# Softmax sums from the value product, reciprocals spread over DRAM, and a narrow maxima row in the last attention

## The chip, the cores and the metric

The kernel runs on one core of one Trainium2 chip. The metric is the device time of one execution, in microseconds (us). The kernel before was timed three times; one further execution was recorded by the hardware profiler, and every row below comes from that one.

## The reference

The reference is two stacks of layers, one after the other, on a sequence of 512 positions and 1024 channels. The change touches only the last mixer of the second stack, a grouped-query attention whose 512 queries see 768 keys (256 of a context and the 512 of the sequence):

```python
def attend(q, k, v):
    q = q.reshape(bsz, lq, A_NKV, A_REP, A_HEADDIM)          # 4 key heads x 4 query heads x 64
    s = jnp.einsum('bqgrd,bkgd->bgrqk', q, k).astype(F32) * (A_HEADDIM ** -0.5)
    p = jax.nn.softmax(s, axis=-1).astype(v.dtype)
    o = jnp.einsum('bgrqk,bkgd->bqgrd', p, v)
    return o.reshape(bsz, lq, A_W)

o_lat = (ol * jax.nn.silu(gl)) @ out_w
```

There are 16 query heads of width 64. Queries and keys are normalised and rotated before this, and scores are large, so the kernel subtracts each query's maximum before the exponential.

## The kernel before

All of it is float32 work done as split products: an operand is kept as a high part (type `fp32r`) and a low part, and three products replace one (`mm3`, lines 229 to 231; `split`, lines 212 and 215). Weights are loaded by SP into one of three `wraw` buffers, split by ScalarE (`whi`, line 212) and by VectorE or, in this attention, GpSimd (`wlo`, line 215).

The last attention is a set of Python generators that are stepped by hand, so that pieces of several jobs alternate in the program. A scheduler then orders each engine's instructions. A chunk `c` is a pair of heads (e = 0 and 1) that share 128 rows; there are 8 chunks, hence 16 turns. In each turn of six steps run:

- `head(c, e)`: for each of 6 blocks of 128 keys, two products give scores minus maximum in PSUM tile `st` (lines 1352, 1353; the second one takes the row of maxima from `qb`). ScalarE takes the exponential twice, once rounded to `fp32r` (`ath`, line 1357) and once in float32 (`ap`, line 1358); VectorE subtracts (`atl`, line 1359). GpSimd adds the `ap` blocks to a running sum `asum` (lines 1362, 1364). Two steps later the block is multiplied with the values: `ath` by [high | low] values into all 128 rows of `po` (line 1370) and `atl` by the high values into 64 rows (lines 1369, 1372). At the end ScalarE and VectorE add both halves of `po` into `aout` (lines 1379, 1380). The first steps of the next turn finish the last two blocks.
- `maxima` of the next head: four times two products fill the one `mx` tile and VectorE reduces it to a column of `a_m` (lines 1328, 1329). VectorE then builds diagonal matrices `adg` of them (line 1332), one product with all-ones rows turns them into a row (line 1336), and ScalarE copies that row into `qb` (line 1337).
- a filler: the gate projection of this chunk (e = 0) or the query projection of the chunk after the next (e = 1), 24 products with `hh` each; towards the end the first output projections (`begin`).
- `finish(c - 1)`, in a turn with e = 0 from its third step: products of `asum` with a column of 2.0 (line 1389; 2, since `agate` holds twice the gate) give sums per query in PSUM tile `aux`, VectorE takes reciprocals (line 1392) and spreads them over a diagonal in `hsq` (line 1394), GpSimd multiplies gate and `aout` (line 1396), products with the identity give the reciprocals in all rows (line 1401), and VectorE multiplies and splits (lines 1402, 215).

PSUM has 8 banks here: one for `mm`, one for `aux`, two for `mx`, two for `st`, two for `po`. After the loop the banks are given out anew and the output projection runs (`fin`, lines 1449 onward): the last chunk's result `ol[7]` is wanted by the last of the eight row blocks of each of its products.

Of the kernel before, what the change touches and what calls it, by code (L numbers as in the profile page):

```python
# [12 lines left out]
F32 = mybir.dt.float32  # L13
F32R = mybir.dt.float32r
AF = mybir.ActivationFunctionType
# [131 lines left out]
class Kern:  # L147
# [1038 lines left out]
    def attention(self, hh, hl, mod):  # L1186
        nc, d = self.nc, self.d
        with ExitStack() as st:
# [11 lines left out]
            vs = ap.tile([P, 6, 2, 256], F32R, name="avs")  # L1200
# [9 lines left out]
            for e in range(2):  # L1210
                for b in range(2):
                    fill(kb[b][e], other[e], 0.0)
                    fill(kb[b][e], row[e], -1.0)
                    fill(qb[b][e], other[e], 0.0)
            tables = ap.tile([P, 2, S], F32, name="rope")
            nc.sync.dma_start(tables, d["rope"].rearrange("e p t -> p e t"))
            onesr = ap.tile([P, P], F32R, name="onesr")
            nc.vector.tensor_copy(onesr, self.ones)
            pick = ap.tile([P, 3], F32, name="two")
            self.two, double = pick[:, :2], pick[:, 2:]  # L1220
            nc.vector.memset(self.two, 0.0)
            nc.vector.memset(double, 2.0)
# [5 lines left out]
            gates, outs = {}, {}  # L1228

# [24 lines left out]
            def values(nb, o, ih, il):  # L1254

                w = [self.weights(d["a_v"][0][:, k * 1024 : (k + 1) * 1024]) for k in range(2)]
                for b in range(nb):
# [6 lines left out]
                    out = vs[:, o + b].rearrange("p g (e f) -> p g e f", f=64)  # L1264
                    self.split(ps[:, :256].rearrange("p (g e f) -> p g e f", g=2, e=2), out[:, :, 0:4:2], out[:, :, 1:4:2])
# [52 lines left out]
            with self.psum(1, 1), self.pool("mx", 1, space=PSUM) as mxp, \  # L1318
                    self.pool("st", 2, space=PSUM) as stp, self.pool("po", 2, space=PSUM) as pop:

                def maxima(c, e):

                    q, k = qa[c % 2][e], ka[c // 4][e]
                    m = self.sp.tile([P, 4], F32, name="a_m")
                    for b in range(4):
                        sc = mxp.tile([P, T], F32, name="mx")
                        for o in (slice(0, S), slice(S, T)):
# [3 lines left out]
                    dg = mp.tile([P, 4, P], F32R, name="adg", bufs=1)  # L1331
                    nc.vector.tensor_tensor(dg, self.ident[:, None, :].to_broadcast([P, 4, P]),
                                            m[:, :, None].to_broadcast([P, 4, P]), op=ALU.mult)
                    yield
                    bc = self.abank()
                    nc.tensor.matmul(bc, onesr, dg.rearrange("p b q -> p (b q)"), start=True, stop=True)
                    nc.scalar.activation(qb[c % 2][e][row[e]], bc[row[e]], AF.Copy)
                    yield

                def head(c, e):  # L1340

                    g, b = c // 4, c % 2
                    both, lead = slice(e * P, (e + 1) * P), slice(e * P, e * P + 64)
                    r = own[e]
                    po = pop.tile([P, S], F32, name="po")
                    total = mp.tile([P, S], F32, name=f"asum{e}", bufs=1)
                    parts = {}
                    for k in range(8):
                        if k < 6:
# [11 lines left out]
                            if k == 1:  # L1361
                                nc.gpsimd.tensor_tensor(total, first, p, op=ALU.add)
                            elif k > 1:
                                nc.gpsimd.tensor_tensor(total, total, p, op=ALU.add)  # L1364
                            first = p
                        if k > 1:
                            th, tl = parts.pop(k - 2)
                            if k == 7:
                                nc.tensor.matmul(po[:64], vs[:, 5, g, lead], tl, start=False, stop=False)
                            nc.tensor.matmul(po, vs[:, k - 2, g, both], th, start=k == 2, stop=k == 7)  # L1370
                            if k < 7:
                                nc.tensor.matmul(po[:64], vs[:, k - 2, g, lead], tl, start=False, stop=False)
                        if k < 7:
                            yield
                    if e == 0:
                        outs[c] = mp.tile([P, S], F32, name="aout", bufs=2), []
                    out, totals = outs[c]
                    totals.append(total)
                    nc.scalar.activation(out[r], po[other[e]], AF.Copy)
                    nc.vector.tensor_tensor(out[r], out[r], po[r], op=ALU.add)  # L1380
                    yield

                def finish(c):

                    out, totals = outs.pop(c)
                    st = self.abank()
                    for b in range(4):
                        for e, total in enumerate(totals):
                            nc.tensor.matmul(st[:, 2 * b + e : 2 * b + e + 1], total[:, b * P : (b + 1) * P], double,  # L1389
                                             start=True, stop=True)  # L1390
                    r = self.sp.tile([P, 8], F32, name="rs_r")
                    nc.vector.reciprocal(r, st[:, :8])
                    dg = mp.tile([P, S], F32, name="hsq", bufs=1).rearrange("p (b q) -> p b q", q=P)
                    nc.vector.tensor_copy(dg.rearrange("p b (e f) -> p (b e) f", e=2), r[:, :, None].to_broadcast([P, 8, 64]))  # L1394
                    t = gates.pop(c)
                    nc.gpsimd.tensor_tensor(t, t, out, op=ALU.mult)
                    yield
                    yield
                    bc = self.abank()
                    for b in range(4):  # L1400
                        nc.tensor.matmul(bc[:, b * P : (b + 1) * P], dg[:, b], self.ident, start=True, stop=True)
                    nc.vector.tensor_tensor(t, t, bc, op=ALU.mult)
                    ol[c] = low(c)
                    self.split(t, oh[c], ol[c])
                    yield
# [131 lines left out]
```

## Time and profile before

| | |
|---|---|
| median of three runs | 3234.89 us (3228.05 to 3239.75) |
| profiled execution, own time | 3230.24 us |
| its span | 3228.5 us |
| TensorE busy (products) | 3075.5 us, 95% |
| VectorE busy | 2050.9 us, 64% |
| ScalarE busy | 1314.0 us, 41% |
| GpSimd busy | 751.0 us, 23% |
| granted TensorE clock, mean | 0.985 |

An engine's busy time counts instructions that run on it; a product's end is modelled, so two products that follow each other closely overlap in the record. The 40 slices of the page are some 81 us each. The last attention's heads lie in the last five of them, where TensorE's digit is 8 instead of 9 and GpSimd's is highest.

### The profile page before, as it was taken

How to read it: one execution, taken by the hardware profiler on the slowest of the kernel's cores; microseconds unless marked ns; L12 is line 12 of the kernel's file. 1: busy time of each engine (PE TensorE's matmuls, PEld its weight loads, DVE VectorE, ACT ScalarE, POOL GpSimd, SP SyncE). 2: the span in 40 equal slices, each digit the busy share in tenths (PEclk: the TensorE clock that was granted, in tenths of full speed). 3: DMA queues.
4: the chain of work that ended last, by engine and by line, in shares of the span. 5: the costliest groups of instructions: out<-in, count | busy, mean ns of one | idle time of the engine just before them, and what ended most of it. 6: DMA issues, size and time to landing. Idle time of an engine off the chain costs nothing. (4 is left out here: it accounts for less than half of the span.)

```text
span 3228.5 us, 39890 instructions
## 1 busy us (share of the span) xinstructions
PE 3075.5 (95%) x15258; PEld 2548.0 (79%) x15258; DVE 2050.9 (64%) x2982; ACT 1314.0 (41%) x2332; POOL 751.0 (23%) x463
## 2 busy tenths in 40 slices
PE   8999999999999999999999999989999989888888
PEld 7888888888888888778788887878888877866667
DVE  6444366444347663577566654878888774768886
ACT  5222235333224442355444433353434443345553
POOL 0000000000002220133002211243333435545664
PEclk9999999999999999999999999999999999989999
DMA  6333322333334443212234444243334435320012
GB/s 198 98 98 93 97 90 74 103 96 95 97 94 151 136 141 107 70 57 64 62 120 142 144 131 146 71 147 102 109 118 137 128 115 160 126 61 25 27 38 82
DMA packets 110465, 334.74 MB, mean 104 GB/s; under 512 B 12329, under 2 KB 21801, under 8 KB 110273
## 3 DMA queue, kind: packets, MB, share of 16 engines
q1 hardware_dynamic: 110272, 332.18, 33.7%
q8 instruction: 120, 1.97, 0.3%
q14 instruction: 73, 0.59, 0.1%
HBM read 320.20 MB, written 11.93 MB: 103 GB/s over the span
## 5 line engine op out<-in xcount | busy, mean ns | idle before, releaser
L229 PE MATMUL mm<-hh,whi 128*128 128x512 f32 x2320 | 915.3, 395 | 7.5 <-DVE bt L1002 5.9
L230 PE MATMUL mm<-hl,whi 128*128 128x512 f32 x2320 | 917.0, 395 | 0.0
L231 PE MATMUL mm<-hh,wlo 128*128 128x512 f32 x2320 | 910.6, 392 | 0.0
L212 ACT ACTIVATE whi<-wraw 128x1024 fp32r<-128x1024 f32 (+3 forms) x414 | 419.2, 1015 | 910.5 <-PE mm L230 593.1
L215 DVE TENSOR_TENSOR wlo<-wraw,whi 128x1024 fp32r<-128x1024 f32 (+2 forms) x345 | 418.5, 1213 | 299.1 <-ACT whi L212 295.6
L229 PEld LDWEIGHTS mm<-hh,whi 128*128 128x128 f32 x2320 | 438.0, 189 | 103.3 <-DVE bt L1002 7.1
L231 PEld LDWEIGHTS mm<-hh,wlo 128*128 128x128 f32 x2320 | 438.2, 189 | 90.8 <-issue 0.2
L230 PEld LDWEIGHTS mm<-hl,whi 128*128 128x128 f32 x2320 | 438.0, 189 | 87.2 <-issue 1.0
L215 POOL TENSOR_TENSOR wlo<-wraw,whi 128x1024 fp32r<-128x1024 f32 x135 | 335.1, 2486 | 482.6 <-DVE whi L214 187.4
L231 PE MATMUL mm<-ah,wlo 128*128 128x512 f32 x704 | 276.5, 393 | 0.0
L229 PE MATMUL mm<-ah,whi 128*128 128x512 f32 x704 | 276.3, 393 | 0.0
L230 PE MATMUL mm<-al,whi 128*128 128x512 f32 x704 | 274.2, 389 | 0.0
L266 POOL TENSOR_TENSOR rs_r<-rs_v,neghalf 128x4 f32<-128x4 f32 (+1 forms) x23 | 25.6, 1114 | 866.9 <-DVE rs_v L265 866.9
L774 POOL TENSOR_TENSOR sq<-sq,wraw 128x512 f32<-128x512 f32 x84 | 122.3, 1456 | 438.4 <-ACT wraw L773 434.8
L339 DVE TENSOR_TENSOR fu<-mm,rbc 128x512 f32<-128x512 f32 x88 | 60.7, 690 | 186.1 <-PE mm L231 185.8
L229 PE MATMUL mm<-ci,whi 128*128 128x256 f32 (+1 forms) x552 | 165.3, 299 | 7.5 <-DVE xf L1002 5.9
L231 PE MATMUL mm<-ci,wlo 128*128 128x256 f32 (+1 forms) x552 | 167.2, 303 | 5.2 <-POOL wlo L215 5.1
L230 PEld LDWEIGHTS mm<-al,whi 128*128 128x128 f32 x704 | 132.2, 188 | 29.9
L231 PEld LDWEIGHTS mm<-ah,wlo 128*128 128x128 f32 x704 | 132.2, 188 | 29.4
L229 PEld LDWEIGHTS mm<-ah,whi 128*128 128x128 f32 x704 | 132.3, 188 | 27.7 <-issue 0.3
L1111 ACT ACTIVATE lb<-lb,nbias 128x128 f32<-128x128 f32 x384 | 120.8, 390 | 56.5 <-POOL lb L1108 56.4
L230 PE MATMUL mm<-ci,whi 128*128 128x256 f32 x464 | 134.5, 290 | 0.0
(486 smaller groups left out, 5080.2 us busy)
## 6 DMA issues: line engine op xcount, KB each, us to landing
wraw<-w_up SPq DMA_DIRECT2D x176, 512.0 KB
wraw<-w_down SPq DMA_DIRECT2D x64, 512.0 KB
wraw<-mod_w SPq DMA_DIRECT2D x48, 512.0 KB
wraw<-m_in SPq DMA_DIRECT2D x48, 512.0 KB
lb<-cum_scr SPq DMA_DIRECT2D x64, 384.0 KB
wraw<-m_out SPq DMA_DIRECT2D x32, 512.0 KB
wraw<-w_down SPq DMA_DIRECT2D x32, 384.0 KB
wraw<-diff_qkv SPq DMA_DIRECT2D x24, 512.0 KB
```

The lines of the kernel that those rows point to most:

```text
L212: nc.scalar.activation(hi, src, AF.Copy)
L215: (rest or nc.vector).tensor_tensor(lo, src, hv, op=ALU.subtract)
L229: mm(ps, ah, bh, start=start, stop=False)
L230: mm(ps, ah, bl, start=False, stop=False)
L231: self.last_mm = mm(ps, al, bh, start=False, stop=stop)
L266: nc.gpsimd.tensor_tensor(r[:, :nb], v[:, :nb], self.neghalf[:, :nb], op=ALU.pow)
L339: nc.vector.tensor_tensor(u, pu, rbc(), op=ALU.mult)
L774: nc.gpsimd.tensor_tensor(acc[1], acc[1], w, op=ALU.add)
L1111: nc.scalar.activation(w[dr][:, c], w[dr][:, c], AF.Exp, bias=nbias[:, c, dr * 32 + h : dr * 32 + h + 1])
```

## The change

`vs`, the tile of values, grows from 256 to 384 columns for each pair of heads: low values of e = 0, high values of e = 0, a block of 2.0, high values of e = 1, a block of zeros, low values of e = 1. A stretch of 128 columns now holds [high | 2.0] or [2.0 | high], so a product with it gives 64 rows of values and 64 rows that all hold twice the sum. Each block of keys takes three products instead of two: `ath` with that stretch, `ath` with the low values (64 columns, or 128 with the zeros), `atl` with that stretch. GpSimd's sums, their tiles and the products of `finish` go away. ScalarE copies the whole `po` into `aout`, one tile for each e.

`finish` now sends the row of 512 sums of each head to a 32 x 32 tile by DMA, VectorE takes 1024 reciprocals at once, a DMA stores them in DRAM (`w_scr`), and two DMAs read them back into 64 rows each (`abc`); one step of the generators lies between these. GpSimd's product of gate and `aout` is in two halves of 64 rows. In `maxima` the diagonal matrices go away, and four products, each with one column of `a_m` as the stationary operand and the identity as the moving one, write the row.

```diff
-            vs = ap.tile([P, 6, 2, 256], F32R, name="avs")
+            vs = ap.tile([P, 6, 2, 384], F32R, name="avs")
...
+            for o, value in ((128, 2.0), (256, 0.0)):
+                for g in range(2):
+                    nc.vector.tensor_scalar(vs[:, :, g, o : o + 64], self.ones[:, None, :64].to_broadcast([P, 6, 64]), value,
+                                            None, op0=ALU.mult)
             tables = ap.tile([P, 2, S], F32, name="rope")
             nc.sync.dma_start(tables, d["rope"].rearrange("e p t -> p e t"))
-            onesr = ap.tile([P, P], F32R, name="onesr")
-            nc.vector.tensor_copy(onesr, self.ones)
-            pick = ap.tile([P, 3], F32, name="two")
-            self.two, double = pick[:, :2], pick[:, 2:]
+            identr = ap.tile([P, P], F32R, name="identr")
+            nc.vector.tensor_copy(identr, self.ident)
+            self.two = ap.tile([P, 2], F32, name="two")
             nc.vector.memset(self.two, 0.0)
-            nc.vector.memset(double, 2.0)
...
+            rscr = self.dr.tile([KC, 2, S], F32, name="w_scr")
...
-                    out = vs[:, o + b].rearrange("p g (e f) -> p g e f", f=64)
-                    self.split(ps[:, :256].rearrange("p (g e f) -> p g e f", g=2, e=2), out[:, :, 0:4:2], out[:, :, 1:4:2])
+                    src = ps[:, :256].rearrange("p (g e f) -> p g e f", g=2, e=2)
+                    for e, (hi, lo) in enumerate(((64, 0), (192, 320))):
+                        self.split(src[:, :, e], vs[:, o + b, :, hi : hi + 64], vs[:, o + b, :, lo : lo + 64])
...
-                    m = self.sp.tile([P, 4], F32, name="a_m")
+                    m = self.sp.tile([P, 4], F32R, name="a_m")
...
-                    dg = mp.tile([P, 4, P], F32R, name="adg", bufs=1)
-                    nc.vector.tensor_tensor(dg, self.ident[:, None, :].to_broadcast([P, 4, P]),
-                                            m[:, :, None].to_broadcast([P, 4, P]), op=ALU.mult)
                     yield
                     bc = self.abank()
-                    nc.tensor.matmul(bc, onesr, dg.rearrange("p b q -> p (b q)"), start=True, stop=True)
-                    nc.scalar.activation(qb[c % 2][e][row[e]], bc[row[e]], AF.Copy)
+                    for b in range(4):
+                        nc.tensor.matmul(bc[:1, b * P : (b + 1) * P], m[:, b : b + 1], identr, start=True, stop=True)
+                    nc.scalar.activation(qb[c % 2][e][row[e]], bc[:1], AF.Copy)
...
-                    both, lead = slice(e * P, (e + 1) * P), slice(e * P, e * P + 64)
-                    r = own[e]
+                    lead, low_ = (slice(64, 192), slice(0, 64)) if e == 0 else (slice(128, 256), slice(256, 384))
+                    rows = slice(0, low_.stop - low_.start)
                     po = pop.tile([P, S], F32, name="po")
-                    total = mp.tile([P, S], F32, name=f"asum{e}", bufs=1)
...
-                            if k == 1:
-                                nc.gpsimd.tensor_tensor(total, first, p, op=ALU.add)
-                            elif k > 1:
-                                nc.gpsimd.tensor_tensor(total, total, p, op=ALU.add)
-                            first = p
                         if k > 1:
                             th, tl = parts.pop(k - 2)
-                            if k == 7:
-                                nc.tensor.matmul(po[:64], vs[:, 5, g, lead], tl, start=False, stop=False)
-                            nc.tensor.matmul(po, vs[:, k - 2, g, both], th, start=k == 2, stop=k == 7)
-                            if k < 7:
-                                nc.tensor.matmul(po[:64], vs[:, k - 2, g, lead], tl, start=False, stop=False)
+                            nc.tensor.matmul(po, vs[:, k - 2, g, lead], th, start=k == 2, stop=False)
+                            nc.tensor.matmul(po[rows], vs[:, k - 2, g, low_], th, start=False, stop=False)
+                            nc.tensor.matmul(po, vs[:, k - 2, g, lead], tl, start=False, stop=k == 7)
...
-                    if e == 0:
-                        outs[c] = mp.tile([P, S], F32, name="aout", bufs=2), []
-                    out, totals = outs[c]
-                    totals.append(total)
-                    nc.scalar.activation(out[r], po[other[e]], AF.Copy)
-                    nc.vector.tensor_tensor(out[r], out[r], po[r], op=ALU.add)
+                    out = mp.tile([P, S], F32, name=f"aout{e}", bufs=1)
+                    nc.scalar.activation(out, po, AF.Copy)
+                    outs.setdefault(c, []).append(out)
...
-                    out, totals = outs.pop(c)
-                    st = self.abank()
-                    for b in range(4):
-                        for e, total in enumerate(totals):
-                            nc.tensor.matmul(st[:, 2 * b + e : 2 * b + e + 1], total[:, b * P : (b + 1) * P], double,
-                                             start=True, stop=True)
-                    r = self.sp.tile([P, 8], F32, name="rs_r")
-                    nc.vector.reciprocal(r, st[:, :8])
-                    dg = mp.tile([P, S], F32, name="hsq", bufs=1).rearrange("p (b q) -> p b q", q=P)
-                    nc.vector.tensor_copy(dg.rearrange("p b (e f) -> p (b e) f", e=2), r[:, :, None].to_broadcast([P, 8, 64]))
-                    t = gates.pop(c)
-                    nc.gpsimd.tensor_tensor(t, t, out, op=ALU.mult)
+                    out, t = outs.pop(c), gates.pop(c)
+                    r = mp.tile([32, 32], F32, name="ars", bufs=1)
+                    for e in range(2):
+                        sums = out[e][other[e].start : other[e].start + 1]
+                        nc.sync.dma_start(r[16 * e : 16 * e + 16], sums.rearrange("o (a b) -> o a b", a=16))
+                    for e in range(2):
+                        nc.gpsimd.tensor_tensor(t[own[e]], t[own[e]], out[e][own[e]], op=ALU.mult)
                     yield
+                    nc.vector.reciprocal(r, r)
+                    nc.sync.dma_start(rscr[c].rearrange("e (a b) -> (e a) b", a=16), r)
                     yield
-                    bc = self.abank()
-                    for b in range(4):
-                        nc.tensor.matmul(bc[:, b * P : (b + 1) * P], dg[:, b], self.ident, start=True, stop=True)
+                    bc = mp.tile([P, S], F32, name="abc", bufs=1)
+                    for e in range(2):
+                        nc.sync.dma_start(bc[own[e]], rscr[c, e].partition_broadcast(64))
+                    yield
                     nc.vector.tensor_tensor(t, t, bc, op=ALU.mult)
```

## Rows read from the trace of the kernel before

**Rows 1.** Windows: start:end, length, busy PE PEld DVE ACT POOL, granted clock, DMA, GB/s
```profile
3004.20:3042.10 37.90, 32.08 (x155) 24.04 (x155) 32.19 (x40) 21.29 (x38) 24.08 (x14) 1.00 0.08 25
...
2865.00:3177.60 312.60, 269.70 (x1238) 202.12 (x1238) 265.03 (x310) 171.08 (x305) 190.11 (x113) 0.97 0.12 33
```

**Rows 2.** Waits of PE, 2865 to 3177.6: total us, times, longest us
```profile
PE mx L1328 <- DVE a_m L1329: 10.5, 9, 1.7
PE po L1372 <- DVE atl L1359: 9.5, 14, 3.8
PE po L1370 <- ACT ath L1357: 6.3, 5, 1.4
PE aux L1389 <- DVE aq L1176: 5.2, 6, 1.0
PE aux L1401 <- DVE hsq L1394: 3.3, 3, 1.1
```

**Rows 3.** Waits of ACT in the same stretch
```profile
ACT aqb L212 <- DVE aq L1184: 21.9, 7, 3.7
ACT ap L1358 <- POOL asum L1362: 20.2, 6, 3.5
```

**Rows 4.** Groups by form, same stretch: shapes xcount | busy us, mean ns | idle before
```profile
L1364 POOL TENSOR_TENSOR asum<-asum,ap 128x512 f32<-128x512 f32 x64 | 103.1, 1610 | 74.0 <-ACT ap L1358 54.5 <-PE mm L231 17.2
L1359 DVE TENSOR_TENSOR atl<-ap,ath 128x512 fp32r<-128x512 f32 x96 | 101.8, 1076 | 6.9 <-ACT ap L1358 6.4
...
L1389 PE MATMUL aux<-two,asum 128*128 128x1 f32 x114 | 13.6, 248 | 5.2 <-DVE aq L1176 5.2
...
L1332 DVE TENSOR_TENSOR adg<-ident,a_m 128x512 fp32r<-128x512 f32 x16 | 12.0, 750 | 0.3
...
L1380 DVE TENSOR_TENSOR aout<-aout,po 64x512 f32<-64x512 f32 x15 | 10.2, 683 | 0.2
...
L1394 DVE COPY hsq<-rs_r 128x512 f32<-128x512 f32 x7 | 10.2, 1456 | 0.0
```

**Rows 5.** Timeline of PE in one step: start us, us, line, what
```profile
3008.98 0.40 PE L1372 MATMUL po<-atl,avs 128*64 128x512 f32 x1
3009.21 0.39 PE L229 MATMUL mm<-hh,whi 128*128 128x512 f32 x1
```

**Rows 6.** Timeline around one `finish`: POOL's sums, DVE beside them and after
```profile
3007.44 3.30 POOL L1364 TENSOR_TENSOR asum<-asum,ap 128x512 f32<-128x512 f32 x2
3007.83 1.77 DVE L1183 TENSOR_TENSOR aq<-aq,rope 128x512 f32<-128x512 f32 x1
...
3011.17 1.13 PE L1401 MATMUL aux<-ident,hsq 128*128 128x128 f32 x8 [1.11 <-DVE hsq L1394]
3011.55 0.68 DVE L1359 TENSOR_TENSOR atl<-ap,ath 128x512 fp32r<-128x512 f32 x1
```

**Rows 7.** Timeline of an earlier stage: a store to DRAM and loads to 128 rows
```profile
2090.30 0.52 SPq L980 DMA_DIRECT2D cum_scr<-row  x1
...
2092.98 0.81 SPq L1106 DMA_DIRECT2D lb<-cum_scr  x2
...
2096.70 0.98 POOL L1108 TENSOR_SCALAR_AFFINE_SELECT lb<-lb 128x768 f32<-128x768 f32 x1 [10.76 <-DMA lb<-cum_scr]
```

**Rows 8.** Waits of SP's queue, 2865 to 3177.6
```profile
SPq L223 <- POOL wlo L215: 276.6, 18, 26.4
```

**Rows 9.** Set-up of the attention: a wait of PE, and fills on DVE
```profile
PE aux L1163 <- DVE two L1224: 2.4, 1, 2.4
...
2812.28 2.52 DVE L1207 TENSOR_SCALAR akb<-ones 64x768 fp32r<-64x768 f32 x5
```

**Rows 10.** Timeline of the end: last `aout`, last `ol`, the first output column's end
```profile
3177.56 0.59 ACT L1379 ACTIVATE aout<-po 64x512 f32<-64x512 f32 x1 [0.65 <-PE po L1370]
...
3183.90 0.69 DVE L215 TENSOR_TENSOR aol<-agate,ci 128x512 fp32r<-128x512 f32 x1 [0.70 <-ACT ci L212]
...
3188.85 0.75 DVE L1457 SCALAR_TENSOR_TENSOR x<-mm,mod,x 128x512 f32<-128x512 f32 x1 [4.26 <-PE mm L231]
```

## The prediction, made before the changed kernel was built

> **What bounds the kernel now.** The page comes first: TensorE is busy 95% of the span, so most of the kernel is bound by products. The slices show where it isn't: the last attention. So the second view is a table of windows over its heads [rows 1]. From 2865 to 3177.6 (312.6 us) TensorE has 269.7 us and stands 42.9; VectorE has 265.0, ScalarE 171.1, GpSimd 190.1. One chunk takes 37.9 us, of which TensorE has 32.1 and VectorE 32.2. Neither is full: they wait for each other in turn.
>
> The third view, TensorE's waits in that stretch [rows 2], names the standstill: 10.5 us for VectorE's maxima (`a_m`), 9.5 for its differences (`atl`), 6.3 for ScalarE's exponentials, 5.2 and 3.3 before the products of `finish`. These 34.8 us are most of the 42.9. ScalarE waits as well [rows 3]: 21.9 us for VectorE's rotated query and 20.2 us for GpSimd, which holds `ap` while it sums.
>
> The fourth view, groups by form, says why VectorE is late [rows 4]. `atl` takes 1076 ns on average. The timeline shows the same operation in 0.68 us where GpSimd rests, and a VectorE product of the same shape in 1.77 us beside two of GpSimd's sums [rows 6]. Over 96 of them that is 96 x 0.39 = 37.8 us. GpSimd's sums are the larger part of GpSimd's time (64 of 80 take 103.1 us, so all some 129 of its 190), so about two thirds of the excess, 25 us, is their doing.
>
> **The change, part by part.**
>
> *Products on TensorE.* Products of 512 columns follow each other at 0.23 us, also after one of 64 columns width [rows 5]. Added: 16 x 6 = 96, at 0.23 us 22.1 us. Also added are 64 narrow maxima products of 128 columns. No row shows a stationary operand one column wide; the nearest is eight products of 128 columns in 1.13 us [rows 6], 0.14 each with the tail, some 0.12 without it; the lower end is nothing, if such short products hide behind others. I take 0.12, as the moving side has the same size: 7.7 us (0 to 9.0). Removed: the products with `asum`, 13.6 us for 114 [rows 4], so 15.3 for 128; the spreads with the identity, 8 x 1.13 = 9.0 us [rows 6]; 16 products for the maxima row, 3.7 us. Net: 22.1 + 7.7 - 28.0 = +1.8 us (-5.9 to +3.1). What looks like a heavy load of new products costs TensorE almost nothing.
>
> A rule speaks against these products. A 64-wide product stands among 128-wide ones now, and its successor starts 0.23 us later, as any other [rows 5]. The Trainium skill (TensorEngine Tiling, Key Properties) says that a change of tiling mode drains the engine. The trace shows no such drain for 64 columns; for one column no run shows it. If the rule held there, my estimate is two changes per head at 0.39 - 0.23 = 0.16 us, 32 x 0.16 = 5 us, and the sum below would be 3216 instead of 3211.
>
> *Work off VectorE.* Gone are `adg` (12.0 us), the adds into `aout` (10.2 for 15, so 10.9) and the spread into `hsq` (10.2 for 7, so 11.7) [rows 4], together 34.6, and some 25 us of slowed `atl`. VectorE falls from 265 to about 205 us. Added: a 32 x 32 reciprocal in place of one over 8 columns, which I count as equal. The last product of `finish` now reads the broadcast from SBUF rather than PSUM, so that it may be slowed by GpSimd as `atl` is: 8 x 1 us at most, which the freed 60 us hide. ScalarE's copy of `po` has twice the rows and the same 512 columns: nothing.
>
> *GpSimd* loses some 129 us and gains 8 products (16 halves for 8 whole ones) at no more than the 1.6 us of a sum [rows 4], 13 us, hidden by its idle time. ScalarE's 20.2 us of waiting for it ends [rows 3], and with it part of TensorE's waits for exponentials.
>
> *TensorE's standstill.* The 8.5 us before the products of `finish` go with them. Of 9.5 for `atl` I leave a third (3), because the weights' low parts still run on GpSimd; of 10.5 for `a_m` half (5), as its one PSUM tile still makes product and maximum alternate; of 6.3 for exponentials half (3); of the rest, 42.9 - 34.8 = 8.1, I leave 5. That is 16 of 42.9, a gain of 27 us. It could be 8 (gain 35) or 30 (gain 13).
>
> *The DMAs.* Each `finish` gets three transfers in a row, with five issues on SP. None of these small ones is in the trace. The nearest: a store to DRAM was issued at 2090.30 and the loads that depend on it at 2092.98, 2.7 us; their broadcast to 128 rows let GpSimd start at 2096.70, 3.7 us [rows 7]. So gather 2.7, store 2.7, broadcast 3.7, with a step of 37.9 / 12 = 3.2 us between each: the first two are covered, the last sticks out by 0.5 us. VectorE, in order, holds back the next `atl` at the reciprocal and at the final product, and TensorE's value products wait behind that. I take 0.4 us per chunk, 3 us (0 to 6; the rest of this case is the second rival). SP's queue stands 276.6 us of this stretch waiting for a free weight buffer [rows 8]; loads queued behind the gather, store and broadcast lose a few us of that, which costs nothing as long as a weight tile is ready two turns ahead.
>
> *Set-up.* TensorE waits 2.4 us for `two`, written by VectorE behind a row of fills [rows 9]. Four fills of the 2.0s and zeros go in front of it. Five fills of 768 columns took 2.52 us, 0.5 each; of 384 columns some 0.3: +1.3 us (0 to 2). Splitting the values in two operations adds six small ones each on ScalarE and VectorE, which stand idle there for longer: nothing (up to 1.8).
>
> *The end.* The last chunk's chain is exposed. Before: `aout` starts at 3177.56 and `ol` is done at 3183.90 + 0.69 = 3184.6 [rows 10], 7.0 us. After: copy 0.6, gather 2.7, store 2.7, broadcast 3.7, then product, high and low part at 0.7 each, 2.1 (the reciprocal between is small beside these): 11.8 us, so 4.8 later. Its first user is the last of eight row blocks of the output product whose end releases VectorE at 3188.85 [rows 10]; three products of 0.23 and a tail before that, about 3187.9, so `ol` lies ready for 3.3 us. Beyond that cover 4.8 - 3.3 = 1.5 us: +1.5 (-3, as TensorE no longer runs 3 us of `finish` products there, to +5, without cover).
>
> *Sum.* -27 + 1.8 + 3 + 1.3 + 1.5 = -19.4 us. The profiled execution took 3230.24 us (span 3228.5 and 1.74 around it), which gives 3211 us. The median of the runs shown is 4.7 us above that execution and their extremes are 12 us apart, which the range has to hold. Ends of this case: -35 - 5.9 - 3 = -44 (3186) and -13 + 3.1 + 6 + 2 + 5 + 1.8 = +5 (3235).
>
> **The rivals.** *TensorE stays held by the alternation.* Turns are kept in order by one `mx` tile and two `st` tiles; if these, and not a slow VectorE, make the waits for `a_m`, `atl` and `ath`, only 8.5 us go: 3230.2 - 8.5 + 1.8 + 3 + 1.3 + 1.5 = 3229 us, no change. For it: VectorE still rests 47 us of 312.6. Against it: ScalarE's 20.2 us for GpSimd and the slowed `atl` are direct and vanish.
>
> *VectorE stands at the DMAs: slower.* Place: the reciprocal and the final product of `finish`. If they are placed in VectorE's order close behind the issues, it stands 2.7 + 6.4 = 9.1 us per chunk, less one covered step of 3.2: 8 x 5.9 = 47 us in place of 3, giving 3211 + 44 = 3255 us. It decides as soon as a transfer takes longer than what VectorE is given to do meanwhile, above 2.4 us exposed per chunk (19.4 / 8) beyond my 0.4. For it: SP issues in order, and a gather that stands behind a weight load waiting up to 26.4 us for its buffer [rows 8] would be late by that. Against it: the three steps add to 9.5 us, about the 9.1 of the transfers, and VectorE gets 60 us of slack.
>
> *The sums were the whole trouble.* If nearly all of the standstill goes (42.9 to 5 us) and the narrow products hide, while DMAs, set-up and end cost their 5.8 us, 3230.2 - 37.9 - 5.9 + 5.8 gives some 3192 us.
>
> **How the numbers follow.** Forecast as summed 0.53, the whole trouble 0.07, the alternation 0.21, VectorE at the DMAs 0.19. The likeliest is 3211 us. The range of 3188 to 3241 leaves out most of the slower case and a little below. A measurement of this kernel can tell about 0.3%, 10 us, from no change. Faster by more: 0.53 + 0.07 less the forecast's upper end (0.04), plus little: 0.57 in all; within: 0.22; slower: 0.21.
>
> **What would show it.** In the profile after: a chunk in about 35 us instead of 37.9; `atl` near 0.8 us on average; ScalarE waiting for no GpSimd sum; TensorE's count of instructions per chunk nearly unchanged and its standstill in the heads below 20 us. VectorE waiting for `ars` or `abc` over 1 us per chunk, or `ol[7]` far behind 12 us after the last `aout`, would point to the second rival. I am wrong if `atl` gets faster and the chunk doesn't, or if weights come late behind the new transfers.

## The result, and the profile after

The changed kernel takes 3190.3 us (median of 3190.0 to 3191.5) beside 3236.6 us of the kernel before on the same chip: ratio 0.986, 95% interval 0.984 to 0.988. The profiled executions are 3230.24 us before and 3190.45 us after, 39.8 us apart. Forecast was 3211 us, a gain of 19.4. The sign and the place were right; the gain is about twice the forecast, and nearly what the rival "the sums were the whole trouble" gave (3192). The time lies 2 us inside the lower end of the stated range (3188 to 3241).

All of it lies in the heads. In the rows PE is TensorE and PEld its weight loads, DVE is VectorE, ACT ScalarE and POOL GpSimd; line numbers are those of the kernel that is read. The windows of the changed kernel: one undisturbed chunk, the heads from 2865 us to the start of the last copy of `po`, and what comes behind it (start:end, length, busy PE, PEld, DVE, ACT, POOL, granted clock, DMA share, GB/s).

```profile
2955.90:2988.40 32.50, 30.87 (x150) 24.35 (x149) 25.31 (x35) 21.04 (x38) 9.40 (x5) 1.00 0.14 41
2865.00:3137.50 272.50, 255.31 (x1213) 201.20 (x1214) 204.66 (x272) 168.00 (x303) 76.40 (x42) 0.99 0.16 47
3137.50:3188.70 51.20, 37.60 (x226) 33.05 (x225) 23.52 (x48) 10.66 (x21) 11.34 (x7) 0.87 0.31 104
```

Against [rows 1]: the heads take 272.5 instead of 312.6 us, a chunk 32.5 instead of 37.9. TensorE stands 17.2 us (272.5 - 255.3) instead of 42.9, and it is busy 14.4 us less. VectorE falls from 265.0 to 204.7 us, GpSimd from 190 to 76. The end is as long as before (51.2 after, 50.9 before).

TensorE's waits in the heads of the changed kernel (total us, times, longest):

```profile
PE po L1368 <- DVE atl L1362: 6.2, 6, 2.6
PE st L1355 <- ACT ap L1361: 6.1, 8, 0.9
PE st L1356 <- ACT aqb L1341: 3.5, 6, 0.6
PE mx L1334 <- DVE a_m L1335: 1.4, 1, 1.4
```

Against [rows 2]: the wait for the maxima `a_m` has gone from 10.5 to 1.4, that for `atl` from 9.5 to 6.2, those for the products of `finish` are gone. ScalarE waits for nothing on GpSimd any more; in [rows 3] it was 20.2 us.

Groups by form in the same stretch (shapes xcount | busy us, mean ns | idle before):

```profile
L1362 DVE TENSOR_TENSOR atl<-ap,ath 128x512 fp32r<-128x512 f32 x96 | 86.8, 912 | 31.4 <-ACT ap L1361 31.0 <-PE po L1368 0.3
...
L1367 PE MATMUL po<-ath,avs 128*64 128x512 f32 (+1 forms) x96 | 37.8, 394 | 0.0
...
L1340 PE MATMUL aux<-identr,a_m 128*1 128x128 f32 x64 | 6.8, 223 | 0.0
...
L1183 DVE TENSOR_TENSOR aq<-aq,rope 128x512 f32<-128x512 f32 x7 | 4.8, 685 | 0.0
```

`atl` has come down from 1076 to 912 ns [rows 4], and VectorE waits 31 us for ScalarE's `ap` where it used to be late itself. The rotation's product with the table, 1.77 us beside GpSimd's sums in [rows 6], takes 0.69.

### The profile page after: what moved, and what is told of

Its sections match the earlier page's. It is cut to its first block, busy times and chain, and to the rows that moved or that the text cites. A ratio compares the mean times of both kernels' runs of the same rounds, so it can differ in the third digit from the quotient of the medians.

```text
span 3188.7 us, 39738 instructions
## 1 busy us (share of the span) xinstructions
PE 3061.8 (96%) x15210; PEld 2547.3 (80%) x15210; DVE 1989.7 (62%) x2951; ACT 1311.9 (41%) x2338; POOL 638.8 (20%) x391
## 5 line engine op out<-in xcount | busy, mean ns | idle before, releaser
L229 PE MATMUL mm<-ah,whi 128*128 128x512 f32 x704 | 276.3, 393 | 0.0
```

The lines of the kernel that those rows point to most:

```text
L229: mm(ps, ah, bh, start=start, stop=False)
```

## The experiments

The table holds for every kernel the median time with that of the kernel before on the same chip, and from its trace the heads (from the start of the first maximum to the start of the last copy of `po`): their length, TensorE's busy and standing time, the granted clock, VectorE's busy time; then what lies behind the last copy. The heads of one kernel may begin some 8 us earlier or later than those of another for reasons that lie ahead of them (2857.1 us in one run, 2873.5 in another, 2865.9 before), so the stretches tell more than the total. Each trace is of one execution: for e9_st3_po1 it is the fastest of four, for e8_no_low_product the slowest.

| kernel | time / before | heads | TensorE busy | stands | clock | VectorE | behind |
|---|---|---|---|---|---|---|---|
| before | 3236.6 | 311.7 | 269.1 | 42.6 | 0.97 | 265.0 | 50.9 |
| after | 3190.3 / 3236.6 | 271.8 | 254.6 | 17.2 | 0.99 | 204.6 | 51.2 |
| e1_narrow_row | 3239.8 / 3234.5 | 319.0 | 276.3 | 42.7 | 0.96 | 256.5 | 50.9 |
| e2_no_sums | 3192.4 / 3234.5 | 270.5 | 261.1 | 9.4 | 0.97 | 214.5 | 49.0 |
| e3_no_finish | 3225.4 / 3234.5 | 311.4 | 262.4 | 49.0 | 0.88 | 262.0 | 46.0 |
| e10_ap4 | 3231.7 / 3233.6 | 311.5 | 268.9 | 42.6 | 0.97 | 265.0 | 50.9 |
| e5_sums_back | 3213.3 / 3232.8 | 297.8 | 263.8 | 34.0 | 0.97 | 242.8 | 51.7 |
| e6_sums_elsewhere | 3254.6 / 3232.8 | 321.2 | 259.8 | 61.4 | 0.91 | 210.0 | 49.5 |
| e6b_sums_paced | 3230.0 / 3233.6 | 308.9 | 269.2 | 39.7 | 0.95 | 216.1 | 54.4 |
| e7_no_dma_chain | 3184.0 / 3232.8 | 271.1 | 254.1 | 17.0 | 1.00 | 200.2 | 46.1 |
| e8_no_low_product | 3176.0 / 3232.8 | 263.0 | 240.9 | 22.1 | 0.99 | 203.4 | 47.2 |
| e9_st3_po1 | 3187.9 / 3234.5 | 271.8 | 255.1 | 16.7 | 0.99 | 204.6 | 50.9 |
| e11_last_local | 3185.2 / 3233.6 | 272.2 | 255.0 | 17.2 | 0.99 | 204.7 | 45.4 |
| e12_row_earlier | 3193.6 / 3233.6 | 283.4 | 261.9 | 21.5 | 0.97 | 201.0 | 46.1 |

The theory: GpSimd's sums were the trouble, since they lengthen VectorE's operations and hold `ap`. The experiments set two other causes against it: the operations taken off VectorE, and the products of `finish` leaving TensorE's queue. The kernels e1, e2, e3 and e10 are made from the kernel before, the others from the changed one.

### Without the sums

```diff
-                            if k == 1:
-                                nc.gpsimd.tensor_tensor(total, first, p, op=ALU.add)
-                            elif k > 1:
-                                nc.gpsimd.tensor_tensor(total, total, p, op=ALU.add)
-                            first = p
...
-                    totals.append(total)
+                    totals.append(self.ones)
```

> The kernel before without GpSimd's 80 sums of exponentials; the eight products of `finish` read a constant in their place, so the softmax denominators are left out of what is computed and every other operation stays. Theory (the sums slow VectorE's differences and hold `ap`): 25 to 40 us less than the kernel before, `atl` near 0.8 us on average, ScalarE no longer waiting for GpSimd. Rival (operations off VectorE): under 10 us, as none of those is removed. Rival (the products of `finish` in TensorE's queue): under 8 us, all from their wait for the sums.

The time falls by 42.1 us (ratio 0.987, 0.985 to 0.989), the heads by 41.2: the whole gain of the change, with none of its other parts. The window of its heads:

```profile
2871.20:3141.70 270.50, 261.13 (x1237) 200.94 (x1235) 214.48 (x310) 169.40 (x302) 63.28 (x34) 0.97 0.13 39
```

Its group of `atl`:

```profile
L1358 DVE TENSOR_TENSOR atl<-ap,ath 128x512 fp32r<-128x512 f32 x96 | 70.1, 742 | 11.6 <-ACT ap L1357 11.2
```

ScalarE's waits, none of them for GpSimd:

```profile
ACT ath L1356 <- PE st L1352: 71.9, 40, 5.5
ACT aqb L212 <- DVE aq L1184: 16.0, 5, 3.2
```

VectorE has the same 310 operations and 50.5 us less to do (265.0 to 214.5): 31.7 of it in `atl`, 14 in the rotation's three operations. TensorE has the same products, stands 33.2 us less, and is busy 8.0 us less. Both other causes are refuted as main ones: here VectorE loses no operation and `finish` keeps its 192 products. It also shows that the rest of the change brings no time: with 34.6 us of operations taken off VectorE besides, the changed kernel's heads are 1.3 us longer than these.

### The narrow row alone

```diff
-                    dg = mp.tile([P, 4, P], F32R, name="adg", bufs=1)
-                    nc.vector.tensor_tensor(dg, self.ident[:, None, :].to_broadcast([P, 4, P]),
-                                            m[:, :, None].to_broadcast([P, 4, P]), op=ALU.mult)
...
-                    nc.tensor.matmul(bc, onesr, dg.rearrange("p b q -> p (b q)"), start=True, stop=True)
+                    for b in range(4):
+                        nc.tensor.matmul(bc[:1, b * P : (b + 1) * P], m[:, b : b + 1], identr, start=True, stop=True)
...
```

> The kernel before with one part of the change alone: the row of maxima comes from four products with a one-column stationary operand, and VectorE's 16 `adg` products (12.0 us) are gone. Theory (the gain came from taking GpSimd's sums away): the sums are still there, so at most 6 us of the 46 us are gained. Rival (it is the operations taken off VectorE that count): 12 us or more, since VectorE is late and each microsecond taken from it is one of the chunk. If the one-column products drain TensorE, TensorE's busy time in the heads grows instead of falling, by 5 us or more.

It is slower: ratio 1.0021 (1.0012 to 1.0030). VectorE has 8.5 us less work, TensorE stands as long as before (42.7 us) and is busy 7.2 us longer, at a clock of 0.96. `atl` stays at 1076 ns. So a microsecond taken off VectorE beside the sums was not one of the chunk. The limit of 5 us of busy time that the expectation set for a drain is passed, but the cause isn't a drain: the 64 narrow products are 7.3 us busy in this run, 0.5 more than the 16 wide ones that they replace (6.8), and in the changed kernel they run like this (start, us):

```profile
3119.40 0.39 PE L1368 MATMUL po<-atl,avs 128*128 128x512 f32 x1
3119.63 0.40 PE L1340 MATMUL aux<-identr,a_m 128*1 128x128 f32 x4
3119.86 0.45 PE L1355 MATMUL st<-aqa,aka 128*128 128x512 f32 x1
```

Four of them take the 0.23 us of one wide product. Most of the rest of the 7.2 us is in the trace. TensorE is busy for 26.9 us at a granted clock of 0.50, where it was 19.3 before: half of the difference, 3.8 us, is lost. And it stops 69 times instead of 56, counting every gap; the last product before a stop counts with its whole 0.40 us and not with the 0.23 to the next one, which makes 13 x 0.17 = 2.2 us.

### Without the reciprocals of `finish`

```diff
-                            nc.tensor.matmul(st[:, 2 * b + e : 2 * b + e + 1], total[:, b * P : (b + 1) * P], double,
-                                             start=True, stop=True)
...
-                    nc.vector.reciprocal(r, st[:, :8])
...
-                    nc.vector.tensor_copy(dg.rearrange("p b (e f) -> p (b e) f", e=2), r[:, :, None].to_broadcast([P, 8, 64]))
...
-                        nc.tensor.matmul(bc[:, b * P : (b + 1) * P], dg[:, b], self.ident, start=True, stop=True)
-                    nc.vector.tensor_tensor(t, t, bc, op=ALU.mult)
```

> The kernel before without the reciprocals of `finish`: its 128 small products, the reciprocal, the spread into `hsq`, the products with the identity and the final product are left out, so the outputs are not divided; GpSimd's sums run as before. Theory (GpSimd's sums): 8 to 18 us less, some 8.5 us of standing and part of the products' 24 us, the rest being taken back by the late `atl` and `a_m`, and `atl` still above 1.0 us. Rival (these products and their waits in TensorE's queue are what the change removed): 28 us less or more, 24 of products and 8.5 of standing.

The time falls by 9 us, but the heads are as long as before (311.4): the gain is behind them (46.0 instead of 50.9). 168 products fewer, and 0.3 us of the heads. TensorE's largest wait of this kernel:

```profile
PE po L1372 <- DVE atl L1359: 34.9, 11, 5.5
```

Four windows of 5 us around one of its turns (columns as above):

```profile
2935.00:2940.00 5.00, 1.79 (x8) 1.12 (x6) 5.00 (x5) 1.99 (x3) 4.84 (x4) 0.93 0.40 105
2940.00:2945.00 5.00, 2.75 (x6) 1.36 (x6) 4.94 (x6) 2.15 (x4) 1.65 (x1) 0.50 0.33 105
2945.00:2950.00 5.00, 3.95 (x10) 2.87 (x11) 4.11 (x5) 2.95 (x7) 1.28 (x1) 0.50 0.00 0
2950.00:2955.00 5.00, 5.00 (x18) 3.82 (x17) 2.18 (x4) 2.98 (x6) 1.78 (x1) 0.71 0.00 0
```

VectorE is full while TensorE is busy 1.8 of 5 us; the wait for `atl` takes the place of the removed products (34.9 us, 9.5 before). During it the granted clock falls to 0.50, its lower level of 1.2 GHz, and stays there for 13.7 us. Seven turns of this kernel have such a wait, of 3.8 to 5.5 us, and in each the clock falls to 0.50 for 6.8 to 13.7 us, mostly 10.2. TensorE is busy for 54.0 us at 0.50, where it was 19.3 before; half of the difference, some 17 us, is lost. So of the 21.2 us of products that are gone from the heads (13.6 + 7.6, lines 1389 and 1401) TensorE's busy time shows only 6.7, and it stands 6.4 us more. These products leaving the queue gain nothing by themselves; what they would be worth at the full clock, this kernel doesn't show.

### Do the sums cost by holding `ap`?

```diff
-                            p = mp.tile([P, S], F32, name="ap", bufs=3)
+                            p = mp.tile([P, S], F32, name="ap", bufs=4)
```

> The kernel before with four `ap` tiles instead of three and nothing else: GpSimd may be one block later with its sums before ScalarE has to wait for it. If the sums cost by holding `ap`: 12 to 25 us less than the kernel before, since most of ScalarE's 20.2 us of waiting for GpSimd goes. If they cost by slowing VectorE's differences: within 6 us of the kernel before, `atl` still above 1.0 us on average.

Ratio 1.0001 (0.9992 to 1.0011). ScalarE's waits in this kernel, from 2865 to 3160 us:

```profile
ACT ath L1357 <- PE st L1353: 81.5, 33, 8.8
ACT aqb L212 <- DVE aq L1184: 39.8, 7, 7.3
```

Its 20.2 us for GpSimd are gone, and the wait for VectorE's rotated query is 39.8 instead of 21.9 [rows 3]: the same idle time under another name. Over the whole heads its waits for the scores, the rotated query and GpSimd are 85.7 + 39.8 + 0 = 125.5 us, where they were 83.0 + 21.9 + 20.2 = 125.1. `atl` stays at 1076 ns and VectorE at 265.0 us. While VectorE is late, holding `ap` costs nothing; this half of the theory falls.

### The sums put back

```diff
...
                             parts[k] = th, tl
+                            for h in range(2 if k else 0):
+                                nc.gpsimd.tensor_tensor(total, p[:, :256], p[:, 256:], op=ALU.add)
```

> The changed kernel with GpSimd's sums put back beside it: five per head, each in two halves of 256 columns that read `ap`; nobody reads the result. Theory (the sums slow VectorE's differences and hold `ap`): 20 to 35 us more than the changed kernel, `atl` back above 1.0 us, ScalarE waiting for GpSimd before `ap` again. Rival (operations off VectorE, and the products of `finish`): under 6 us more.

23 us more than the changed kernel, 26.0 in the heads. VectorE's operations are the same 272 and take 38.2 us more. The window of the heads:

```profile
2865.90:3163.70 297.80, 263.75 (x1211) 205.09 (x1210) 242.82 (x272) 168.66 (x302) 225.29 (x199) 0.97 0.13 43
```

The group of `atl`:

```profile
L1363 DVE TENSOR_TENSOR atl<-ap,ath 128x512 fp32r<-128x512 f32 x96 | 114.2, 1197 | 24.8 <-ACT ap L1362 23.9
```

TensorE's waits:

```profile
PE st L1356 <- ACT ap L1362: 13.1, 8, 1.9
PE po L1371 <- DVE atl L1363: 9.5, 6, 3.0
PE mx L1334 <- DVE a_m L1335: 6.8, 6, 1.9
```

ScalarE doesn't wait for GpSimd here, against the expectation, and VectorE's wait for GpSimd's `rs_r` is 12.1 us as in the changed kernel (12.0); the lengthened operations of VectorE are what is left. In the kernel before the lengthening can be watched in the timeline. VectorE:

```profile
3020.78 4.77 DVE L1359 TENSOR_TENSOR atl<-ap,ath 128x512 fp32r<-128x512 f32 x3
```

GpSimd in the same time:

```profile
3018.77 2.85 POOL L215 TENSOR_TENSOR wlo<-wraw,whi 128x1024 fp32r<-128x1024 f32 x1
3021.58 1.73 POOL L1362 TENSOR_TENSOR asum<-ap 128x512 f32<-128x512 f32 x1
3023.39 1.62 POOL L1364 TENSOR_TENSOR asum<-asum,ap 128x512 f32<-128x512 f32 x1
```

Three differences of 0.68 us each take 4.77 us, and go in step with three operations of GpSimd. Counted over all 96 of the kernel before by what lies longest beside each: the 26 with no GpSimd operation beside them take 0.68 us on average, the 44 beside a sum 1.26, the 15 beside a weight's low part (`wlo`) 1.43. The Trainium skill (SBUF — State Buffer, Who interferes with whom) calls the shared port pair an exclusive lock for a VectorE instruction with two SBUF inputs beside a GpSimd instruction that reads SBUF. These rows agree, and so does `a_m`, which has one input in PSUM and takes 0.95 us in every kernel here.

### The sums on tiles of their own

First without any tie to the heads, then each pair started by one column of that block's `atl` (the second diff):

```diff
...
+                            for h in range(2 if k else 0):
+                                nc.gpsimd.tensor_tensor(total, total, total, op=ALU.add)
```

```diff
...
+                            if k:
+                                nc.gpsimd.tensor_tensor(total[:, :1], tl.bitcast(F32)[:, :1], tl.bitcast(F32)[:, :1], op=ALU.add)
+                                for h in range(2):
+                                    nc.gpsimd.tensor_tensor(total, tables[:, 0, :256], tables[:, 1, :256], op=ALU.add)
```

> The same additional GpSimd sums in the changed kernel, as many and as wide, but on a tile of their own, so that they hold no `ap`. If the sums cost by slowing VectorE's operations: the same time as with the sums of `ap`, within 5 us, `atl` above 1.0 us. If they cost by holding `ap`: within 5 us of the changed kernel. Rival (the sums are not what counts): within 3 us of the changed kernel in both.

> The changed kernel with as many additional GpSimd sums on tiles of their own as before, now each pair started by one column of that block's `atl`, so that they run beside the head and not in bunches of up to 32 us, and hold no `ap`. If the sums cost by slowing VectorE: 15 to 30 us more than the changed kernel, `atl` above 1.0 us. If they cost by holding `ap`: within 6 us of the changed kernel.

Both are far slower than the changed kernel, by 64 and 40 us, and neither meets an expectation. What slows them isn't what was to be measured: VectorE is only 5.4 and 11.5 us busier, and in the first kernel only 9 of the 96 differences lie beside a sum. The first kernel, timeline of GpSimd in the first head:

```profile
2917.86 32.41 POOL L1367 TENSOR_TENSOR asum<-asum 128x256 f32<-128x256 f32 x42
```

VectorE's wait for GpSimd in its heads:

```profile
DVE hsq L1170 <- POOL rs_r L1168: 37.7, 7, 27.2
```

The second kernel, VectorE's and TensorE's waits:

```profile
DVE hsq L1170 <- POOL rs_r L1168: 32.8, 7, 6.3
...
PE mx L1335 <- DVE a_m L1336: 22.6, 8, 3.7
```

GpSimd also makes `rs_r`, a small operation for the query's norm that VectorE waits for. With 42 sums, or with sums that wait for `atl`, ahead of it in GpSimd's order, VectorE stands 37.7 and 32.8 us (12.0 in the changed kernel), and TensorE behind it. That is a second price of work on GpSimd; before, this wait was 6.7 us, so it isn't what the change removed. The two runs don't isolate the lengthening by itself. `atl` takes 979 ns where the sums start behind it and 1197 ns where the same `ap` releases both; that the order of start makes the difference is not shown, as the operands differ too.

### Without the transfers of `finish`

The five transfers are left out, with constant tiles in place of `ars` and `abc`.

> The changed kernel without the five transfers of `finish`: the reciprocal and the final product read constant tiles, so the outputs are not divided by their sums; every other operation stays. Theory (the transfers are covered in the heads and by the row blocks of the output product at the end): within 3 us of the changed kernel. Rival (they hold VectorE back): 6 us less or more.

6 us less by the medians (ratio 0.985, 0.984 to 0.986, an interval that overlaps that of the changed kernel); in the traces the heads are 0.7 shorter, the end 5.1. In the heads the transfers cost next to nothing, as expected; at the end they are not covered. There VectorE waits for both (changed kernel; start, us, and the wait in brackets):

```profile
3143.40 0.34 DVE L1388 RECIPROCAL ars<-ars 32x32 f32<-32x32 f32 x1 [6.51 <-DMA ars<-aout]
3148.65 0.69 DVE L1395 TENSOR_TENSOR agate<-agate,abc 128x512 f32<-128x512 f32 x1 [4.91 <-DMA abc<-w_scr]
```

### Without the 96 added products

```diff
-                            nc.tensor.matmul(po[rows], vs[:, k - 2, g, low_], th, start=False, stop=False)
```

> The changed kernel without the 96 products of the values' low parts, so the value product is less exact; every other operation stays. If TensorE's own time is now the bound: some 96 x 0.23 = 22 us less. If the alternation with VectorE and ScalarE still is: under 8 us less, and the standstill grows by the rest.

Between the two: TensorE is busy 13.7 us less in the heads and stands 4.9 us more, 8.8 in all. The end is another 4 us shorter, though no product was removed there; 2 of these are VectorE's waits for the last transfers (2.5 and 7.0 us for the 6.5 and 4.9 above), the rest stays open. A product less is worth some 0.09 us in the heads (8.8 / 96) where 0.23 would be expected of a TensorE that is its own bound. The turns of the engines still count after the change.

### Three score tiles

```diff
-                    self.pool("st", 2, space=PSUM) as stp, self.pool("po", 2, space=PSUM) as pop:
+                    self.pool("st", 3, space=PSUM) as stp, self.pool("po", 1, space=PSUM) as pop:
```

> The changed kernel with three score tiles in PSUM and one tile for the value product instead of two and two. Theory (what is left of TensorE's standstill is the wait for a score tile, 9.6 of 17.2 us, while `po` is emptied by one short copy): 3 to 8 us less than the changed kernel. Rival (the one `po` tile makes the next head's value products wait for ScalarE's copy): the same time or up to 8 us more.

The heads take the same 271.8 us and only begin earlier (2857.1 us). The total, 2.4 us less by the medians, is no different within its spread (3181.6 to 3194.1). TensorE's waits:

```profile
PE po L1368 <- DVE atl L1362: 6.9, 8, 1.6
PE mx L1334 <- DVE a_m L1335: 6.3, 3, 2.2
PE st L1356 <- ACT aqb L1341: 3.5, 6, 0.6
```

The 6.1 us for a score tile are gone and the maxima wait 6.3 instead of 1.4. The rival's time came out, but not its reason: the wait went on to `mx`, not to `po`.

### The last chunk without transfers, and the row one step earlier

```diff
+                    if c == KC - 1:
+                        bc = mp.tile([P, S], F32, name="abc", bufs=1)
+                        for e in range(2):
+                            nc.scalar.activation(bc[own[e]], out[e][other[e]], AF.Copy)
+                        nc.vector.reciprocal(bc, bc)
```

and in the second kernel also

```diff
                         yield
-                    yield
                     bc = self.abank()
```

> The changed kernel with the last chunk's reciprocals made in place: ScalarE copies the sums, which stand in 64 rows of each copied tile, to the other half, and VectorE takes the reciprocals of 128 x 512 and multiplies; no transfer. The 7 chunks before keep their transfers. Theory (the transfers cost only at the end, 6.5 and 4.9 us of VectorE's waiting there): the stretch behind the last copy falls from 51.2 to 46 or 48 us, the time by 3 to 6 us. Rival (the wide reciprocal, about 3.3 us, takes their place): within 2 us of the changed kernel.

> The kernel of the run before this, with the row of maxima one step earlier: the narrow products need no VectorE product before them, so the empty step that was kept for it goes. Theory (TensorE's 3.5 us of waiting for `aqb` come from the row being late): another 2 to 5 us less, and no wait for `aqb`. Rival (TensorE now waits for the last maximum instead): the same time, with the wait at the narrow products grown by what goes at the scores.

The first has the lowest median of the kernels here that compute all: 3185.2 us (3182.4 to 3186.9), ratio 0.9853 (0.9838 to 0.9868). Its heads are unchanged (272.2) and its end is 45.4 instead of 51.2 us. The interval overlaps that of the changed kernel, so it is the stretch that shows the gain. Its reciprocal of 512 columns:

```profile
3139.27 3.35 DVE L1386 RECIPROCAL abc<-abc 128x512 f32<-128x512 f32 x1 [1.93 <-ACT abc L1385]
3142.73 0.69 DVE L1403 TENSOR_TENSOR agate<-agate,abc 128x512 f32<-128x512 f32 x1
```

The product starts 4.7 us behind the last copy (11.1 in the changed kernel).

The second loses 11.2 us in the heads again. No wait for `aqb` is left, and instead:

```profile
PE mx L1334 <- DVE a_m L1335: 15.2, 7, 3.1
```

The rival held in kind, and its price is larger than what was saved: most of the wait is at the next maxima, not at the narrow products (1.5 us), and the clock falls from 0.99 to 0.97.

## Why the prediction was right, and where its sizes were off

*What bounds the kernel.* Right: the gain is all in the mutual waits of the heads, and the 2865 us ahead of them are as before.

*The standstill.* 42.9 to 16 was forecast, 42.9 to 17.2 measured: -25.7 for -27. That the sum fits so well is in part luck, as its parts were off one by one: `a_m` 1.4 for 5 left, `atl` 6.2 for 3, exponentials 0 for 3, scores 9.6 where 5 were left for all the rest.

*Products on TensorE: the step that failed.* +1.8 us was forecast, and the busy time fell by 14.4. By counts the term is near: the 96 products stand 0.23 us apart, as forecast, 22.1; the 64 narrow ones take 0.23 for four, 3.7 instead of 7.7. The 28.0 that was taken off also holds the eighth `finish`, which runs behind the heads; inside them 13.6 + 7.6 + 3.7 = 24.9 us of products are gone, so that the counts give +0.9. The other 15 us are in no count: the forecast had no term for what else makes TensorE's busy time. The trace shows two such things.

One is the clock. These are the stretches of the heads in which it was at 0.50, five of the kernel before and one of the changed kernel (columns as above):

```profile
2891.60:2895.00 3.40, 3.38 (x8) 2.45 (x9) 3.37 (x4) 2.50 (x5) 2.79 (x2) 0.50 0.00 0
2901.80:2908.60 6.80, 5.67 (x18) 4.90 (x19) 6.09 (x8) 0.00 (x0) 2.20 (x2) 0.50 0.27 77
3045.20:3048.60 3.40, 3.40 (x9) 2.54 (x8) 3.40 (x3) 0.60 (x1) 3.23 (x3) 0.50 0.00 0
3082.70:3086.10 3.40, 3.40 (x10) 2.65 (x10) 3.40 (x3) 0.60 (x1) 3.24 (x3) 0.50 0.00 0
3120.30:3123.70 3.40, 3.40 (x10) 2.51 (x9) 3.40 (x3) 0.60 (x1) 3.24 (x3) 0.50 0.00 0
...
2898.90:2902.30 3.40, 2.95 (x9) 2.47 (x10) 2.48 (x4) 0.00 (x0) 0.00 (x0) 0.50 0.33 131
```

TensorE was busy in them for 19.3 us before and for 2.95 after; at the full clock half of the difference would do, so some 8 us come back. The forecast had the 0.97 among its rows and gave it no term. The other is the number of stops. The last product before a stop counts with its full 0.40 us and not with 0.23, so that each stop costs some 0.17 more than its standing. Counting every gap, TensorE stops 56 times in the heads before and 21 times after: 35 x 0.17 = 6 us. Together with the +0.9 that is some -13 of the -14.4. Without the sums, with no product changed, the busy time fell by 8.0 us in the same way: 30 stops, and 13.7 us busy at 0.50.

*The drain at each change of tiling mode*, by the rule of the Trainium skill (TensorEngine Tiling (Array Packing), Key Properties), would have made it 3216. No row shows one: a product of 64 columns, four of one column and the next of 128 follow each other at 0.23 us.

*Work off VectorE.* 265 to 205 was forecast, 204.7 measured, but two errors cancel, which is luck. The sums alone take 50.5 us from it, not 25: `atl` loses 31.7 of its 37.8 us of excess, and the rotation, for which there was a row of 1.77 us, was not counted at all over its 8 chunks (14 us). And in the changed kernel `atl` still takes 912 ns, not 0.8 us, as GpSimd's `wlo` (2.29 us each) and its gate products (1.42) lie beside it: the 65 differences with nothing of GpSimd beside them take 0.69 us on average, the 16 beside `wlo` 1.45, the 15 beside a gate product 1.32. The forecast put the gate products, now 15 of 64 rows instead of 7 of 128, down as hidden.

*GpSimd and `ap`.* ScalarE's wait went as forecast, but it was no part of the gain: the fourth `ap` tile removed it for nothing.

*The DMAs.* +3 was forecast, 0 measured (heads 0.7 us shorter without them). They are covered as the row of 2.7 and 3.7 us suggested; the second rival's VectorE at the transfers is 0.6 us in the seven inner chunks.

*Set-up.* +1.3 forecast, by a longer wait for `two`; that wait is still 2.4 us. The heads begin at 2865.7 instead of 2865.9, which tells little, as their begin varies by some 8 us.

*The end.* +1.5 forecast, +0.3 measured. `ol` is done at 3150.73, 13.2 us behind the last copy (11.8 forecast). The +0.3 is a balance of two larger amounts: without the last chunk's transfers the end is 5.8 us shorter, and about as much is saved there by what `finish` no longer runs (without its reciprocals the end of the kernel before was 4.9 shorter).

*The rivals.* The alternation (3229) is refuted as the cause of the old standstill, but it is what remains: 96 products less bring 8.8 us instead of 22, and three score tiles move a wait without removing it. "The sums were the whole trouble" got 0.07 and came nearest. Its mechanism is the one that the runs show, though by another sum: 17 us of standing stayed, and the busy time made up for it.

## What to carry to other kernels

When two engines wait for each other, look first for what lengthens the late one's operations: an operation that takes 0.68 us alone and 1.1 on average names its neighbour, and taking the neighbour away gained 41 us of the heads where taking 8.5 us of other work off the late engine gained nothing. A wait on the page (20 us of ScalarE for GpSimd) is no gain until something shows that nothing else was late at that point; one more buffer tells it in one run. And the standing time of TensorE isn't all that its waits cost: of the 14.4 us that its busy time fell, some 6 went with 35 stops and some 8 with the time at the lower clock, so a forecast needs a term for both.

## What the runs showed of the hardware that was not expected

In the kernel without the reciprocals of `finish` the granted clock falls to 0.50 in each of seven waits of 3.8 to 5.5 us, for 10.2 us in most of them; of the 21.2 us of products that were taken out of its heads, some 17 came back as time at the lower clock. VectorE's reciprocal takes 3.35 us for 128x512 and 0.34 us for 32x32, so 6.5 and 10.6 ns per column, where a product of 128x512 takes 0.69 us, 1.3 per column. Four products with one stationary column together cost TensorE the time of one wide product, 0.23 us.
